# The scan step ahead of the inverse step in each slot of a chunked DeltaNet recurrence

## The chip, the cores and the metric

The kernel runs on one core of a Trainium2 chip. The metric is the time of one execution on the device, in microseconds (us). Three executions of the kernel before took 1556.57, 1556.83 and 1557.63 us; their median, 1556.83 us, is the time to be compared with.

## What is computed

One layer of a hybrid trunk over 1024 tokens of width 1024: RMSNorm, one input projection, a gated DeltaNet mixer with 8 heads beside 4 heads of cross-attention to 256 memory tokens, an output projection, and a SwiGLU feed-forward block of width 2816. The change touches the DeltaNet mixer, whose core in the reference is (cut):

```python
sol = triangular_solve(lower + eye, rhs, lower=True, unit_diagonal=True)   # per chunk
u, w = sol[..., :DV], sol[..., DV:]
def step(state, xs):                       # over the chunks, in order
    v_new = u_n - w_n @ state
    o_n = qg_n @ state + p_n @ v_new
    state = state * gl_n + kg_n.T @ v_new
    return state, o_n
```

The kernel works with chunks of 128 tokens, so that a head has 8 of them. A triangular matrix of each chunk is inverted first (this needs no state); then the chunks of a head are gone through one after the other.

## The kernel before

**Units and iterations.** A unit is one head and one half of the sequence, four chunks; there are 16 units. The loop over `i` runs 20 iterations. In iteration `i` three things stand side by side: the dense input projection for unit `i` (products of 128x128 weights with 128x512 inputs, each done three times with split operands; accumulator `pj`), the inverse of unit `i - 1` (the generator `inverse`), and the recurrence of unit `i - 2` (the generator `scan`). Iterations 2 to 15 have all three; 16 and 17 have no projection of the mixer left.

**Slots.** An iteration is cut into 16 slots. A slot takes one step of `inverse`, one step of `scan`, the small helpers that the table `STEPS` puts there (transposes of keys, values and queries, the chunk systems), one `tap` (a conv multiply-add on VectorE, tile `cv`, L295), and two steps of the projection, which are six 128x512 products on TensorE (one step in iteration 15).

**Steps of `inverse`** (fp16, four chunks at once). Even slots 0 to 10: a product `pz` of 64 columns per chunk, then VectorE masks it into a tile `zlev` (L517). Odd slots 1 to 11: products `pT` (from `zlev`) and `pU`, then VectorE adds them into `T` (L530) and `U` (L532). Slots 12 to 14: products `pe`, `pv`, `pv2` of 128 columns that correct the result to `uf`. Slot 15 has none.

**Steps of `scan`** (fp32, one chunk per four slots). First slot: product `pc` of state and keys, then VectorE makes `r` (L592). Second: product `pc<-r,uf`, then `vn` (L597). Third: product `pc<-vn,kg`, then the new state `st` (L606). Fourth: the output `po`. An fp32 product of 128x128 is two passes on TensorE; the profile shows it as x2. A unit that begins a head has no product in slot 0, one that ends a head none in slot 14.

**What sets the order.** In iterations 2 to 15 the small products are kept on TensorE in the order in which the program issues them (`pinned`), with the projection between them. On VectorE a scheduler places the instructions, but a `tap` goes behind `crit[0]`, the VectorE instruction that `inverse` or `scan` issued last. In iterations 16 and later the scheduler orders TensorE too.

The loop of the slots (L718 to L731, cut):

```python
for s in range(SLOTS):
    if s == SLOTS - 1:
        stage(k_first, i)
    next(inv, None)
    next(scn, None)
    for fn, lag in STEPS.get(s, ()):
        ...
        stage(fn, i + lag)
    if s in TAPS:
        tap()
    for _ in range(per):
        next(work, None)
```

Of the kernel before, what the change touches and what calls it, by code (L numbers as in the profile page):

```python
# [54 lines left out]
def trunk_kernel(ctx: ExitStack, tc: tile.TileContext, a: dict, out: bass.AP):  # L55
# [224 lines left out]
    def conv_silu(ct_i):  # L280

        cb = pp.tile([P, S + 4], F32, tag="cb", name="cb")
        nc.gpsimd.memset(cb[:, 0:4], 0.0)
        cv = pp.tile([P, NT, P], F32, tag="cv", name="cv", bufs=4)
        w = convw[:, ct_i, :]

        def half(hf, pj):
            cf = flat(cv)[:, hf * HF:(hf + 1) * HF]
            nc.scalar.copy(cb[:, 4 + hf * HF:4 + (hf + 1) * HF], pj)
            nc.scalar.activation(cf, pj, AF.Copy, scale=w[:, 3:4])  # L290

            def taps():
                for j in (2, 1, 0):
                    c0 = 1 + j + hf * HF
                    nc.vector.scalar_tensor_tensor(out=cf, in0=cb[:, c0:c0 + HF], scalar=w[:, j:j + 1],  # L295
                                                   in1=cf, op0=ALU.mult, op1=ALU.add)
                    if j == 0:
                        nc.scalar.activation(cf, cf, AF.Silu)
                    yield
            pending.append(taps())  # L300
        return cv, half
# [3 lines left out]
    def tap():  # L305

        while pending:
            with behind():
                if next(pending[0], 0) is None:
                    return  # L310
            pending.pop(0)
# [31 lines left out]
    def dense(jobs):  # L343

        for dst, key, make in jobs:
            whi, wlo = next_w()
            dst[key], half = make()
            for hf in range(2):
                pj = bank("pj", "pj")
                for dt in range(ND):  # L350
                    w, v = whi[:, dt, :], wlo[:, dt, :]
                    x, y = uhi[hf][:, dt, :], ulo[hf][:, dt, :]
                    mm(pj, w, x, start=dt == 0, stop=False)
                    mm(pj, w, y, start=False, stop=False)
                    mm(pj, v, x, start=False, stop=dt == ND - 1)
                    if dt == ND - 1:
                        half(hf, pj)
                    yield
# [287 lines left out]
    def weight_sums(k):  # L646

        def load(i, j):
            t = pp.tile([P, HF], F32, tag="kvo", name="wsum", bufs=3)
            nc.sync.dma_start(t, wo_block(i, j, k))  # L650
            return t

        def put(name, dst, x, y):
            nc.gpsimd.tensor_tensor(out=dst, in0=x, in1=y, op=ALU.subtract)
            nc.sync.dma_start(t_d[name][k], dst)

        b12, b11 = load(1, 2), load(1, 1)
        put("T1", b11, b12, b11)
        b22 = load(2, 2)
        put("T3", b12, b22, b12)  # L660
        put("T2", b22, b22, b11)
        b21 = load(2, 1)
        put("T4", b21, b21, b22)

    def stage(fn, u):
        if 0 <= u < 2 * H:
            return fn(u // 2, u % 2, hd[u // 2], st[u])
# [36 lines left out]
    for i in range(2 * H + 4):  # L704
        h = i // 2
        jobs = []
        if h < H:
            if i % 2 == 0:
                jobs = [(hd[h], "vT", lambda h=h: conv_silu(16 + h)), (hd[h], "qT", lambda h=h: conv_silu(h))]
            else:  # L710
                if h + 1 < H:
                    jobs = [(hd[h + 1], "kT", lambda h=h: conv_silu(9 + h))]
                jobs += [(hd[h], "zs", silu_z)]
        pinned[0] = 2 <= i < 2 * H
        work = dense(jobs)
        per = len(jobs) * 2 * ND // SLOTS
        inv, scn = stage(inverse, i - 1) or iter(()), stage(scan, i - 2) or iter(())
        for s in range(SLOTS):  # L718
            if s == SLOTS - 1:
                stage(k_first, i)  # L720
            next(inv, None)
            next(scn, None)
            for fn, lag in STEPS.get(s, ()):
                if fn is post and i == 2 * H - 1:
                    continue
                if fn is post_y and i >= 2 * H - 1:
                    continue
                stage(fn, i + lag)
                if fn is q_scores and i == 2 * H:
                    with tc.issue_after(st[i - 1]["qk_ins"]):  # L730
                        stage(post_y, i - 4)  # L731
                        stage(post_y, i - 3)
                if fn is k_system and i == 2 * H - 1:
                    with tc.issue_after(st[i]["al_ins"]):
                        stage(post, i - 3)
# [4 lines that stand above are left out]
        for _ in work:  # L740
            pass
        if i % 2 == 1 and 1 <= h <= KH:
            with tc.issue_after(st[i]["al_ins"]), tc.issue_after(st[i]["gr_ins"]):
                weight_sums(h - 1)
# [703 lines left out]
def build(arrays):  # L1448
    import concourse.bacc as bacc

    nc = bacc.Bacc("TRN2", target_bir_lowering=False, num_devices=1)
    aps = {}
    for name, v in arrays.items():
        aps[name] = nc.dram_tensor(f"in_{name}", v.shape, mybir.dt.from_np(v.dtype), kind="ExternalInput").ap()
    out = nc.dram_tensor("out_h", (S, D), F32, kind="ExternalOutput").ap()
    with tile.TileContext(nc) as tc:  # L1456
        trunk_kernel(tc, aps, out)
    return nc
# [9 lines left out]
```

## Time and profile before

| | |
|---|---|
| median of three executions | 1556.83 us |
| the profiled execution, its own time | 1557.43 us |
| its span, first to last instruction | 1555.3 us |
| TensorE (PE) busy over the span | 1477.7 us, 95% |
| VectorE (DVE), ScalarE (ACT), GpSimd (POOL) busy | 69%, 44%, 53% |
| mean granted TensorE clock | 0.986 of full speed |
| iterations 2 to 15 | 130.5 to 614.5 us of the span |

The profiled execution's time is its span and 2.1 us around it. PE counts products, PEld the loading of their stationary operand, which runs beside PE. In a timeline a row is an instruction, or several equal ones (xN), with its start and its length; the starts of pipelined products tell more than their lengths, which overlap. A bracket at a row's end is idle time of the engine just before, and what ended it.

### The profile page before, as it was taken

Reading aid. Unit: us, or ns where it says so; the run is one execution under the profiler, and the core shown is the slowest. Engines: PE = TensorE matmul, PEld = TensorE weight load, DVE = VectorE, ACT = ScalarE, POOL = GpSimd, SP = SyncE. Lnnn points to the kernel's source line nnn. Section 1 sums busy time; section 2 is a strip of 40 time slices with the busy share of each in tenths; the row PEclk is TensorE's granted clock in tenths of the full one; section 3 lists DMA queues with packets and bytes.
Section 4 is the critical chain, followed back from the end, with each engine's and each line's share of the span. In section 5 each row is a group of like instructions: output and inputs, shape, how many; then the busy total and the mean of one; then the engine's idle time right before and its main releaser. Section 6 shows DMA issues by size and latency. Waiting matters only on the chain. (4 is left out here: it accounts for less than half of the span.)

```text
span 1555.3 us, 22654 instructions
## 1 busy us (share of the span) xinstructions
PE 1477.7 (95%) x8237; PEld 1180.3 (76%) x8237; DVE 1067.9 (69%) x1651; ACT 680.4 (44%) x1481; POOL 822.4 (53%) x705
## 2 busy tenths in 40 slices
PE   7999999999999999999898889999999999999996
PEld 5777777777777777887676668877887887778784
DVE  7565766656666757667977886666766766585967
ACT  7464445455454554345346532222222222544352
POOL 3543636464546544204755556666656565544455
PEclk9999999999999999999899899999999999999998
DMA  6411213122212220219334222222222324973334
GB/s 201 156 55 42 77 53 104 68 76 64 85 62 76 76 74 29 82 62 306 108 109 148 81 94 97 102 102 100 103 86 93 112 81 144 317 251 98 93 97 161
DMA packets 77554, 168.13 MB, mean 108 GB/s; under 512 B 10434, under 2 KB 12930, under 8 KB 77443
## 3 DMA queue, kind: packets, MB, share of 16 engines
q1 hardware_dynamic: 76720, 165.58, 31.9%
q8 instruction: 64, 1.05, 0.3%
q10 hardware_dynamic: 722, 1.12, 0.2%
q14 instruction: 48, 0.39, 0.1%
HBM read 124.42 MB, written 42.24 MB: 107 GB/s over the span
## 5 line engine op out<-in xcount | busy, mean ns | idle before, releaser
L246 PE MATMUL pj<-uhi,whi 128*128 128x512 f32 x496 | 215.7, 435 | 0.0
L93 POOL TENSOR_TENSOR wlo<-raw,whi 128x1024 fp32r<-128x1024 f32 x61 | 158.2, 2594 | 74.9 <-ACT whi L92 74.6
L246 PE MATMUL pj<-uhi,wlo 128*128 128x512 f32 x496 | 195.8, 395 | 0.0
L246 PE MATMUL pj<-ulo,whi 128*128 128x512 f32 x496 | 193.7, 391 | 0.0
L1292 POOL TENSOR_TENSOR wlo<-ar,whi 128x512 fp32r<-128x512 f32 x75 | 105.4, 1407 | 99.8 <-ACT whi L1291 99.8
L295 DVE SCALAR_TENSOR_TENSOR cv<-cb,convw_sb,cv 128x512 f32<-128x512 f32 x144 | 132.6, 921 | 24.0 <-ACT cv L290 23.3
L907 PE MATMUL fo<-wlo,whi 128*128 128x512 f32 x308 | 123.0, 399 | 9.4 <-DVE wlo L1292 9.2
L92 ACT CAST whi<-raw 128x1024 fp32r<-128x1024 f32 x66 | 69.6, 1055 | 119.2 <-DVE raw L1057 56.7
L908 PE MATMUL fo<-whi,wlo 128*128 128x512 f32 x308 | 120.6, 392 | 0.0
L906 PE MATMUL fo<-whi 128*128 128x512 f32 x308 | 118.4, 391 | 0.6 <-DVE c L854 0.6
L1095 DVE TENSOR_TENSOR raw<-raw 128x512 f32<-128x512 f32 x86 | 100.3, 1167 | 23.7 <-POOL wlo L93 13.7
L1292 DVE TENSOR_TENSOR wlo<-B,whi 128x512 fp32r<-128x512 f32 x75 | 80.9, 1081 | 45.9 <-ACT whi L1291 45.3
L246 PEld LDWEIGHTS pj<-uhi,wlo 128*128 128x128 f32 x496 | 93.1, 188 | 21.5 <-POOL wlo L93 0.2
L1057 DVE TENSOR_TENSOR raw<-raw,gcols_sb 128x1024 f32<-128x1024 f32 x44 | 64.1, 1457 | 57.9 <-DMA raw<-in_w_ffn_in 57.5
L246 PEld LDWEIGHTS pj<-ulo,whi 128*128 128x128 f32 x496 | 94.2, 190 | 10.8
L246 PEld LDWEIGHTS pj<-uhi,whi 128*128 128x128 f32 x496 | 94.0, 189 | 10.7 <-issue 0.2
L1291 ACT CAST whi<-ar 128x512 fp32r<-128x512 f32 x75 | 46.6, 621 | 113.1 <-POOL wlo L1292 75.4
L530 DVE TENSOR_TENSOR T<-pT,T 128x256 f16<-128x256 f32 x96 | 40.6, 423 | 59.5 <-PE pT L246 58.8
L907 PE MATMUL acc<-wlo,whi 128*128 128x512 f32 x168 | 68.7, 409 | 12.6 <-DVE wlo L891 12.6
L907 PEld LDWEIGHTS fo<-wlo,whi 128*128 128x128 f32 x308 | 58.2, 189 | 29.3 <-DVE wlo L1292 17.7
L1078 POOL TENSOR_TENSOR qlo<-raw,qhi 128x1024 fp32r<-128x1024 f32 x21 | 54.8, 2611 | 42.9 <-ACT qhi L1077 38.5
L517 DVE TENSOR_TENSOR zlev<-pz,lvmask_sb 128x256 f16<-128x256 f32 x96 | 40.4, 421 | 47.1 <-PE pz L246 47.0
(408 smaller groups left out, 4250.9 us busy)
## 6 DMA issues: line engine op xcount, KB each, us to landing
raw<-in_w_ffn_in SPq DMA_DIRECT2D x44, 512.0 KB, 3.3
raw<-in_w_in SPq DMA_DIRECT2D x36, 512.0 KB, 3.2
ar<-g_S SPq DMA_DIRECT2D x44, 256.0 KB, 2.6
B<-in_w_ffn_out SPq DMA_DIRECT2D x42, 256.0 KB, 4.6
g_A<-g SPq DMA_DIRECT2D x33, 256.0 KB, 2.0
ar<-g_A SPq DMA_DIRECT2D x29, 256.0 KB, 3.8
wsum<-in_w_out SPq DMA_DIRECT2D x24, 256.0 KB, 4.3
T_d<-wsum SPq DMA_DIRECT2D x24, 256.0 KB, 2.0
```

Of the source, the lines that this page charges most:

```text
L92: nc.scalar.copy(hi, raw)
L93: (lo_eng or nc.gpsimd).tensor_tensor(out=lo, in0=raw, in1=hi.bitcast(F32), op=ALU.subtract)
L246: ins = nc.tensor.matmul(*args, **kw)
L295: nc.vector.scalar_tensor_tensor(out=cf, in0=cb[:, c0:c0 + HF], scalar=w[:, j:j + 1], in1=cf, op0=ALU.mult, op1=ALU.add)
L906: nc.tensor.matmul(acc[n], hi[:, 0, ts_], hi[:, 1], start=first, stop=False)
L907: nc.tensor.matmul(acc[n], hi[:, 0, ts_], lo[:, 1], start=False, stop=False)
L908: return nc.tensor.matmul(acc[n], lo[:, 0, ts_], hi[:, 1], start=False, stop=last)
L1057: nc.vector.tensor_tensor(out=raw, in0=raw, in1=gcol[:, 1, :].unsqueeze(2).broadcast_to([P, ND, P]), op=ALU.mult)
L1078: nc.gpsimd.tensor_tensor(out=lo, in0=src, in1=hi.bitcast(F32), op=ALU.subtract)
L1095: nc.vector.tensor_tensor(out=o, in0=x, in1=y, op=op)
L1291: nc.scalar.copy(hi[:, i], src)
L1292: last_lo[i] = eng.tensor_tensor(out=lo[:, i], in0=src, in1=hi[:, i].bitcast(F32), op=ALU.subtract).ins
```

## The change

Two lines change places, so that in every slot of every iteration the step of `scan` is issued ahead of the step of `inverse`.

```diff
@@ -718,8 +718,8 @@
         for s in range(SLOTS):
             if s == SLOTS - 1:
                 stage(k_first, i)
+            next(scn, None)
             next(inv, None)
-            next(scn, None)
             for fn, lag in STEPS.get(s, ()):
                 if fn is post and i == 2 * H - 1:
                     continue
```

No instruction is added or taken away. On GpSimd and on the DMA queue of SyncE the order of instructions stays the same. On TensorE, in slot 10 of one iteration, before (`pj` is the projection, `pk` a transpose that a helper issues; the three further pairs of `ah` and `pz` are left out):

```order
L246 MATMUL pj<-uhi_127,wlo 128x512
L246 LDWEIGHTS ah
L246 MATMUL pz<-T,ah 128x64
...
L246 MATMUL pc<-vn,kg 128x128
L250 MATMUL pk<-ident_sb,cv 128x128 x4
L246 MATMUL pj<-uhi_127,whi 128x512
```

On TensorE, the same slot now:

```order
L246 MATMUL pj<-uhi_127,wlo 128x512
L246 MATMUL pc<-vn,kg 128x128
L246 LDWEIGHTS ah
L246 MATMUL pz<-T,ah 128x64
...
L250 MATMUL pk<-ident_sb,cv 128x128 x4
L246 MATMUL pj<-uhi_127,whi 128x512
```

The fp32 product of the scan stood between the fp16 products and the transpose; now it stands between the projection and the fp16 products.

On VectorE, from slot 9 to the start of slot 11 of an iteration, before (`cv` is a tap, `zlev_433` the mask tile of the last level):

```order
L530 TENSOR_TENSOR T<-pT,T 128x8x32
L532 TENSOR_TENSOR U<-pU,U 128x8x32
L295 SCALAR_TENSOR_TENSOR cv<-cb,convw_sb,cv 128x512
L597 TENSOR_SCALAR vn<-pc,beta 128x128
L295 SCALAR_TENSOR_TENSOR cv<-cb,convw_sb,cv 128x512
L517 TENSOR_TENSOR zlev_433<-pz,lvmask_sb 128x4x64
L606 SCALAR_TENSOR_TENSOR st<-st,eg_tot,pc 128x128
```

On VectorE, the same place now:

```order
L597 TENSOR_SCALAR vn<-pc,beta 128x128
L530 TENSOR_TENSOR T<-pT,T 128x8x32
L295 SCALAR_TENSOR_TENSOR cv<-cb,convw_sb,cv 128x512
L532 TENSOR_TENSOR U<-pU,U 128x8x32
L295 SCALAR_TENSOR_TENSOR cv<-cb,convw_sb,cv 128x512
L606 SCALAR_TENSOR_TENSOR st<-st,eg_tot,pc 128x128
L517 TENSOR_TENSOR zlev_433<-pz,lvmask_sb 128x4x64
```

`vn` came behind `T`, `U` and a tap and now leads; `zlev_433` came behind three instructions of the slot before and now has `st` ahead of it too.

## Rows read from the trace of the kernel before

**Rows 1.** Busy time by stage: iterations 2 to 15, then the two after.

```profile
core 0: us, PE busy (x) PEld busy (x) DVE busy (x) ACT busy (x) POOL busy (x), PEclk, DMA share, GB/s
130.50:614.50 484.00, 477.25 (x3580) 379.26 (x3580) 316.44 (x676) 247.04 (x655) 254.65 (x283) 1.00 0.21 70
614.50:645.00 30.50, 30.50 (x258) 25.45 (x255) 19.70 (x50) 10.75 (x43) 11.57 (x17) 1.00 0.22 69
```

**Rows 2.** Waits of PE in 130.5:614.5: us in total, times, longest.

```profile
PE pc L246 <- DVE vn L597: 5.2, 15, 1.0
```

**Rows 3.** Timeline of PE, slots 8 to 11 of one iteration.

```profile
217.45 0.40 PE L246 MATMUL pj<-uhi,wlo 128*128 128x512 f32 x1
...
218.35 0.39 PE L246 MATMUL pj<-ulo,whi 128*128 128x512 f32 x1
...
219.26 0.40 PE L246 MATMUL pj<-uhi,wlo 128*128 128x512 f32 x1
219.50 0.29 PE L246 MATMUL pT<-zlev,U 128*128 128x64 f16 x4
...
221.45 0.29 PE L246 MATMUL pz<-T,ah 128*128 128x64 f16 x4
222.04 0.49 PE L246 MATMUL pc<-vn,kg 128*128 128x128 f32 x2 [0.30 <-DVE vn L597]
...
224.20 0.29 PE L246 MATMUL pT<-zlev,U 128*128 128x64 f16 x4
```

**Rows 4.** Timeline of PE, a slot with transposes (slot 4).

```profile
207.95 0.40 PE L246 MATMUL pj<-uhi,wlo 128*128 128x512 f32 x1
208.19 0.29 PE L246 MATMUL pz<-T,ah 128*128 128x64 f16 x4
208.32 0.47 PE L246 MATMUL pc<-st,khT 128*128 128x128 f32 x2
208.62 0.60 PE L250 MATMUL pvt<-ident_sb,cv 128*128 128x128 f32 x4
...
209.29 0.40 PE L246 MATMUL pj<-ulo,whi 128*128 128x512 f32 x1
```

**Rows 5.** Timeline of PE in iteration 16, where scan precedes inverse.

```profile
623.27 0.39 PE L135 MATMUL pj<-uhi,whi 128*128 128x512 f32 x1
623.50 0.38 PE L246 MATMUL pc<-st,khT 128*128 128x128 f32 x2
623.72 0.39 PE L246 MATMUL po<-st,gr 128*128 128x128 f32 x2
623.94 0.28 PE L246 MATMUL pz<-T,ah 128*128 128x64 f16 x4
...
624.38 0.39 PE L137 MATMUL pj<-uhi,wlo 128*128 128x512 f32 x1
```

**Rows 6.** Timeline of PE in iteration 1: transposes right behind inverse, no scan.

```profile
104.83 0.29 PE L246 MATMUL pz<-T,ah 128*128 128x64 f16 x4
...
105.65 0.39 PE L246 MATMUL pj<-ulo,whi 128*128 128x512 f32 x1
```

**Rows 7.** Timeline of DVE, the stretch of rows 3.

```profile
219.83 0.42 DVE L530 TENSOR_TENSOR T<-pT,T 128x256 f16<-128x256 f32 x1 [1.13 <-PE pT L246]
220.17 0.41 DVE L532 TENSOR_TENSOR U<-pU,U 128x256 f16<-128x256 f32 x1
220.50 1.22 DVE L295 SCALAR_TENSOR_TENSOR cv<-cb,convw_sb,cv 128x512 f32<-128x512 f32 x1
221.64 0.34 DVE L597 TENSOR_SCALAR vn<-pc,beta 128x128 f32<-128x128 f32 x1
221.90 1.38 DVE L295 SCALAR_TENSOR_TENSOR cv<-cb,convw_sb,cv 128x512 f32<-128x512 f32 x1
223.21 0.41 DVE L517 TENSOR_TENSOR zlev<-pz,lvmask_sb 128x256 f16<-128x256 f32 x1
```

**Rows 8.** Timeline of POOL, the stretch of rows 3.

```profile
221.13 1.61 POOL L489 TENSOR_TENSOR al<-at,ah 128x512 f16<-128x512 f32 x1
```

**Rows 9.** All taps (L295): ns min/median/max, first and last start in us.

```profile
L295 DVE SCALAR_TENSOR_TENSOR cv<-cb,convw_sb,cv x144: 735/750/2890, 36.8 to 597.7; 128x512 f32<-128x512 f32 x144
```

## The prediction

> **What bounds the kernel now.** I read the busy times by stage first. In iterations 2 to 15, the only stretch where the two generators run beside the projection on a fixed order, PE is busy for 477.25 of 484.00 us; VectorE is busy for 316.44 us, ScalarE and GpSimd for about half, and the granted clock is 1.00, the 2.4 GHz level [rows 1]. PE is the bound, and time can be won in two ways only: by the 6.75 us in which PE sits idle, and by how closely its products follow each other, which busy time hides, since pipelined products overlap. So the second view is who PE waited for: most of it is one wait, the scan's product `pc<-vn,kg` for the VectorE result `vn`, 15 times, 5.2 us [rows 2]. The third is the timeline of one such wait, with PE and VectorE beside each other [rows 3, 7]. The fourth is the distance from the start of the last dense product of a slot to the second one of the next: I call it the bridge, and it is what the small products cost PE [rows 3 to 6].
>
> **The wait in slot 10.** In slot 9 VectorE does `T`, `U`, a tap and only then `vn`. The tap took 1.22 us where the median tap takes 0.75 [rows 7, 9], so `vn` ended at 221.98 (221.64 + 0.34). In slot 10 PE was at `pz` at 221.45; the scan's product follows a `pz` by 0.13 (208.19 to 208.32 [rows 4]), so it could have started at 221.58 and started at 222.04 [rows 3]. That is 0.46 lost, of which the bracket shows 0.30; the other 0.16 is the modelled tail of `pz`. For 15 waits: 5.2 + 15 x 0.16 = 7.6 us. After the change `vn` stands ahead of `T`. Its product starts 0.23 behind the last dense one (623.27 to 623.50 [rows 5]), at 219.49, and is 0.38 long, so `vn` runs from about 219.91 to 220.25, where PE wants it at 221.43. The margin is over a microsecond. **Term 1: 7.6 us less.**
>
> **The bridges.** Each slot now goes dense, scan, inverse, helpers, dense; it went dense, inverse, scan, helpers, dense. No trace of before shows the new bridge whole in iterations 2 to 15, but its pieces stand in iterations 16 and 1. Dense to scan 0.23; a two-pass fp32 product to the next fp32 product 0.22 (623.50 to 623.72), and from fp32 to `pz` the same 0.22 (623.72 to 623.94); `pz` to the second dense product 0.44 (623.94 to 624.38) [rows 5]; `pz` through four transposes to the second dense product 0.82 (104.83 to 105.65) [rows 6].
> A slot without helpers: before 217.45 to 218.35, 0.90 [rows 3]; after 0.23 + 0.22 + 0.44 = 0.89. A slot with four transposes: before 207.95 to 209.29, 1.34 [rows 4]; after 0.23 + 0.22 + 0.82 = 1.27. The reason shows in one distance: a scan product behind fp16 products takes 0.30 to its successor (208.32 to 208.62 [rows 4]), behind a dense one 0.22 [rows 5]. The loading of its stationary operand is covered by a dense product and not by the short fp16 ones. Afterwards an uncovered load remains, but where transposes follow it is a cheaper one.
> Transposes follow in slots 2, 4, 5 and 10, in 14 iterations less one without a next key: 55 slots x 0.07 = 3.9 us. Of the other eleven slots with an inverse step, slot 0 of seven units and slot 14 of seven have no scan product: 154 - 14 = 140 slots x 0.01 = 1.4 us. The starts are rounded to 0.01, so a slot may be off by 0.02: 0.05 to 0.09 and 0 to 0.03, together 2.8 to 9.2 us. I take the differences as they stand. **Term 2: 5.3 us less.**
>
> The Trainium skill speaks against term 2: "TensorE: Matmul & The Clock Gate", section "Step-by-step: what each phase is for", says that PE pulls the load of a stationary operand ahead of the running matmul, so that the next weights load while this one computes. By that rule alone the order inside a slot would cost nothing and term 2 would be zero. The distances agree with it beside dense products and not beside the fp16 ones of 64 columns.
>
> **A new wait, slot 11.** What was early becomes late: `T` and the mask `zlev` now stand behind the scan's VectorE step. The tightest place is `zlev_433`, which `pT` of slot 11 needs. By rows 7: `vn` holds VectorE for 0.26 (221.64 to 221.90), so `T` starts at 220.17 instead of 219.83; `T` 0.34, tap 1.14 (220.50 to 221.64), `U` 0.33, tap 1.31 (221.90 to 223.21), `st` 0.26 like `vn`, `zlev` 0.41: it ends at 223.96, and PE sees it some 0.06 later (221.98 to 222.04), at 224.02. PE: slot 10 starts at 221.43, lasts 2.75 - 0.46 - 0.07 = 2.22 (221.45 to 224.20 [rows 3], less the wait and the shorter bridge), so slot 11 starts at 223.65; its output product is four passes, 0.44 (623.50 to 623.94 [rows 5]), and `pT` comes at 224.09. The slack is 0.07 us, a knife edge, once in each of 14 iterations. I take 0.5 us in all (some units late by less than 0.1); the ends are 0 and the price in the first rival. **Term 3: 0.5 us more.** Elsewhere the scan's VectorE step delays `T` or `zlev` by no more than 0.34, and `pz` or `pT` needs them most of a slot (219.50 to 221.45 [rows 3]) later.
>
> **What costs nothing.** The tap stays behind the last step of the slot, whichever generator issued it. GpSimd and the DMA queue keep their order, and PE waits for neither of them here; GpSimd's 254.65 us fit into a stage of 471 as well. In iterations 16 and 17 the scheduler orders anew, but PE was busy for all of 30.50 us [rows 1], with projection products of the memory heads as filler; I allow 1 us either way. Behind them PE's program is as before and the whole is 95% PE, so what is won arrives at the end.
>
> **The sum.** -7.6 - 5.3 + 0.5 = -12.4 us. The profiled execution took 1557.43 us, which gives 1545.0; it is 0.6 above the median, so against that I predict **1544.4 us**, 0.8% less.
>
> **The rivals.**
> *Late mask.* The two taps run beside GpSimd's `al` (221.13 to 222.74 [rows 8]) and were 0.47 and 0.63 longer than the median. If their new place costs another 0.47 (what the first one lost), `zlev_433` is 0.40 late: 14 x 0.40 = 5.6 in place of 0.5, so 1549.5. For it: the margin of 0.07. Against: the second tap starts only 0.08 later, and `al` ends while it runs. The Trainium skill, "SBUF — State Buffer", section "SBUF: two separate sides", says that the port pair shared by VectorE and GpSimd is an exclusive lock and the loser blocks for the whole instruction. By it the second tap would start when `al` ends, at 222.74, and end 0.2 later than I have it: 14 x 0.13 = 1.8 us for term 3, 1545.7. The first tap, 0.75 of work done in 1.22 while GpSimd was busy throughout, speaks against a full block. Chance 0.18, with all between.
> *The loads are covered anyway.* Term 2 is zero, because scan products behind dense ones wait for something that iteration 16 doesn't show: 1556.83 - 7.6 + 0.5 = 1549.7. The distances of [rows 5, 6] speak against it. Chance 0.09. The rule of the Trainium skill named under term 2 ends at the same time.
> *The change doesn't do what it says.* The order of PE shows that it does; but if both the wait merely moves (from `vn` to `zlev_433`, 0.46 each) and the bridges stay, nothing is left: 1556.8. Chance 0.04.
> *VectorE becomes the bound: slower.* Place: the two taps between slots 9 and 11. Taps of up to 2.89 us occur [rows 9]. If the second took that long instead of 1.38, `zlev_433` would be 1.51 - 0.07 = 1.44 late in each unit: +20.2 - 12.9 = +7.3, 1564.1. It turns from a gain to a loss at (7.6 + 5.3) / 14 + 0.07 = 1.0 us of lateness. Against: VectorE has 167 us free in the stage, and nothing on GpSimd grows. Chance 0.04.
>
> **How the numbers follow.** The forecast, with its rounding (2.8 to 9.2 in term 2), has 0.65. The range goes from 1541.5 (term 2 at 8) to 1550.5, which takes in the late mask and the covered loads; it leaves out the last two rivals and the far ends. A difference under 0.2% (3.1 us) can't be told from none. Faster by more than that: 0.65 + 0.18 + 0.09 - 0.01 for a double mishap = 0.91; within: 0.05; slower: 0.04.
>
> **What would show it.** Right: the wait for `vn` gone from PE's list; bridges of 1.27 in slots 2, 4, 5 and 10; the stage 130.5 to 614.5 shorter by some 12 us and what follows as long as before. Term 1 is wrong if another wait of about 0.4 stands in slot 10 or 11; term 2 if the bridges with transposes are still 1.34; term 3 shows as PE waiting for `zlev` L517 fourteen times. If the stage wins 12 us and the end doesn't, the gain was given back behind 645.

## The result, and the profile after

| | before | after |
|---|---|---|
| median of four executions each | 1557.07 us | 1535.97 us |
| lowest and highest | 1556.57, 1557.63 | 1533.81, 1536.47 |
| the profiled execution's span | 1555.3 us | 1533.7 us |

The ratio is 0.9866, with an interval of 0.9837 to 0.9896: 21.1 us less, 1.3%. The forecast was 12.4 less, and the time lies below its range. To see where the other 9 us come from, I cut both spans at the starts of the same products:

| stretch of the span, us | before | after | difference |
|---|---|---|---|
| up to iteration 2 | 127.4 | 129.1 | +1.7 |
| iterations 2 to 15 | 487.1 | 476.2 | -10.9 |
| iterations 16 and 17, memory attention | 84.5 | 83.6 | -0.9 |
| output projection (`acc`) | 155.0 | 153.6 | -1.4 |
| from there to the FFN loop | 42.8 | 41.9 | -0.9 |
| FFN loop, first product of `T3` to first `fo` | 420.5 | 412.4 | -8.1 |
| output of the FFN | 238.0 | 237.0 | -1.0 |

(The cut of iterations 2 to 15 begins 3 us ahead of that in the table of before, so it is 487 and not 484.) The stage of the forecast gave 10.9 us and the two iterations behind it 0.9, near the 12.4 of the forecast. The surprise lies 300 us behind them, in a loop that the change doesn't touch.

**The stage of the slots, after.** Busy time by stage (us; each engine's busy time and instructions, granted clock, DMA share, GB/s), to be laid beside [rows 1]:

```profile
core 0: us, PE busy (x) PEld busy (x) DVE busy (x) ACT busy (x) POOL busy (x), PEclk, DMA share, GB/s
132.20:605.20 473.00, 470.42 (x3583) 405.95 (x3582) 331.70 (x676) 246.05 (x655) 256.05 (x283) 1.00 0.22 72
605.20:634.80 29.60, 29.60 (x256) 24.87 (x254) 20.17 (x50) 10.50 (x42) 11.59 (x17) 1.00 0.21 67
```

Here 11.0 us are gone, 4.2 of them idle time of PE, the rest in the distances that busy time hides. All waits of PE in that stretch (us in total, times, longest), beside [rows 2]:

```profile
PE pz L246 <- DVE T L530: 1.6, 1, 1.6
PE pT L246 <- DVE zlev L517: 0.7, 1, 0.7
PE pc L246 <- DVE vn L597: 0.2, 1, 0.2
```

The fifteen waits for `vn` are one, and `zlev` is waited for once and not fourteen times. The timeline of PE, slots 8 to 11 of the same iteration as in [rows 3] (start, length):

```profile
216.90 0.40 PE L246 MATMUL pj<-uhi,wlo 128*128 128x512 f32 x1
217.13 0.39 PE L246 MATMUL pc<-st,khT 128*128 128x128 f32 x2
217.35 0.28 PE L246 MATMUL pz<-T,ah 128*128 128x64 f16 x4
...
217.78 0.40 PE L246 MATMUL pj<-ulo,whi 128*128 128x512 f32 x1
...
220.65 0.39 PE L246 MATMUL pj<-uhi,wlo 128*128 128x512 f32 x1
220.87 0.38 PE L246 MATMUL pc<-vn,kg 128*128 128x128 f32 x2
221.09 0.28 PE L246 MATMUL pz<-T,ah 128*128 128x64 f16 x4
221.21 0.63 PE L250 MATMUL pk<-ident_sb,cv 128*128 128x128 f32 x4
...
221.91 0.39 PE L246 MATMUL pj<-ulo,whi 128*128 128x512 f32 x1
...
223.05 0.38 PE L246 MATMUL po<-st,gr 128*128 128x128 f32 x2
...
223.50 0.28 PE L246 MATMUL pT<-zlev,U 128*128 128x64 f16 x4
```

The bridge of slot 8 is 216.90 to 217.78, 0.88; that of slot 10, with its transposes, 220.65 to 221.91, 1.26. VectorE beside it:

```profile
219.37 0.35 DVE L597 TENSOR_SCALAR vn<-pc,beta 128x128 f32<-128x128 f32 x1 [1.13 <-PE pc L246]
219.64 0.41 DVE L530 TENSOR_TENSOR T<-pT,T 128x256 f16<-128x256 f32 x1
219.97 1.20 DVE L295 SCALAR_TENSOR_TENSOR cv<-cb,convw_sb,cv 128x512 f32<-128x512 f32 x1
...
222.92 0.41 DVE L517 TENSOR_TENSOR zlev<-pz,lvmask_sb 128x256 f16<-128x256 f32 x1
```

`vn` is done at 219.72, 1.1 us before PE wants it (220.87). The mask ends at 223.33 and `pT` starts at 223.50; the knife edge of the forecast held.

**The FFN loop, before and after.** The waits of PE for the low half `qlo` of the next weights, 900 to 1330 us, first in before, then in after:

```profile
PE sc L137 <- POOL qlo L1078: 10.8, 7, 3.5
```

```profile
PE sc L137 <- POOL qlo L1078: 3.5, 1, 3.5
```

Of the 8.1 us of the loop 7.3 are in this one wait. The groups of line L1095, four VectorE steps per block that combine the weights, same stretch (count | busy us, mean ns | idle time ahead and what ended it), before and then after:

```profile
L1095 DVE TENSOR_TENSOR raw<-raw 128x512 f32<-128x512 f32 x80 | 94.9, 1186 | 23.4 <-POOL wlo L93 13.7 <-POOL wlo L1078 8.6
```

```profile
L1095 DVE TENSOR_TENSOR raw<-raw 128x512 f32<-128x512 f32 x80 | 79.4, 992 | 25.4 <-POOL wlo L93 17.1 <-POOL wlo L1078 7.1
```

The same 80 instructions, on the same data, in a loop whose order is the same on every engine in both traces, take 15.5 us more in before. One block of each shows why. Before, VectorE and GpSimd:

```profile
976.55 0.69 DVE L854 TENSOR_TENSOR c<-g,v 128x512 f32<-128x512 f32 x1 [1.19 <-POOL g L854]
977.16 2.90 DVE L1095 TENSOR_TENSOR raw<-raw 128x512 f32<-128x512 f32 x1
979.99 0.68 DVE L854 TENSOR_TENSOR u<-iv,m 128x512 f32<-128x512 f32 x1
...
976.58 2.93 POOL L1078 TENSOR_TENSOR plo<-raw,phi 128x1024 fp32r<-128x1024 f32 x1
983.87 3.07 POOL L1078 TENSOR_TENSOR qlo<-raw,qhi 128x1024 fp32r<-128x1024 f32 x1 [4.36 <-PE pj L137]
```

After:

```profile
965.07 0.68 DVE L1095 TENSOR_TENSOR raw<-raw 128x512 f32<-128x512 f32 x1
965.67 0.68 DVE L854 TENSOR_TENSOR u<-iv,m 128x512 f32<-128x512 f32 x1
...
965.73 2.42 POOL L1078 TENSOR_TENSOR plo<-raw,phi 128x1024 fp32r<-128x1024 f32 x1 [1.30 <-ACT phi L1077]
969.56 2.40 POOL L1078 TENSOR_TENSOR qlo<-raw,qhi 128x1024 fp32r<-128x1024 f32 x1 [1.41 <-ACT qhi L1077]
```

In before the fourth step of L1095 starts 0.58 us behind GpSimd's `plo`, takes 2.90 us instead of 0.68 and ends 0.55 behind it; `u<-iv,m`, which PE's next products need, comes 2.2 us later. In after the fourth step has just ended when `plo` starts. I call such a meeting a collision. In before 7 of the 18 blocks behind block 3 have one of over 2 us, and the starts of `plo` follow each other by anything from 18.2 to 23.0 us, mostly 18.4 and 21.3 in turn; in after there is none, and they follow each other by 19.2 us, block for block. Seven collisions for 8.1 us of loop are 1.2 us each. So the question for the experiments was: does the slot order cause the collisions, or does it only happen to go with them?

### The profile page after: what moved, and what is told of

Its sections match the earlier page's. It is cut to its first block, busy times and chain, and to the rows that moved or that the text cites. A ratio compares the mean times of both kernels' runs of the same rounds, so it can differ in the third digit from the quotient of the medians.

```text
span 1533.7 us, 22655 instructions
## 1 busy us (share of the span) xinstructions
PE 1468.6 (96%) x8237; PEld 1207.5 (79%) x8237; DVE 1068.4 (70%) x1651; ACT 682.1 (44%) x1481; POOL 825.6 (54%) x705
## 3 DMA queue, kind: packets, MB, share of 16 engines
q8 instruction: 64, 1.05, 0.3%
## 4 chain that ended last, share of the span: by engine, by line
PE 35%; DVE 5%; POOL 4%; issue 3%; DMA 2%; ACT 2%; DVEq 0%; SPq 0%; POOLq 0%; ACTq 0%
PE fo L907 3%; PE fo L908 3%; PE fo L906 3%; PE sc L137 3%; PE sc L135 2%; PE sc L136 2%; PE iv L135 2%; PE iv L137 2%; PE iv L136 2%; PE pj L136 2%; PE pj L137 2%; PE pj L135 2%; POOL wlo L891 2%; DVE B L854 1%; PE ms L136 1%
## 5 line engine op out<-in xcount | busy, mean ns | idle before, releaser
L295 DVE SCALAR_TENSOR_TENSOR cv<-cb,convw_sb,cv 128x512 f32<-128x512 f32 x144 | 148.3, 1030 | 23.1 <-ACT cv L290 22.4
L1095 DVE TENSOR_TENSOR raw<-raw 128x512 f32<-128x512 f32 x86 | 84.8, 986 | 25.6 <-POOL wlo L93 17.1
L1057 DVE TENSOR_TENSOR raw<-raw,gcols_sb 128x1024 f32<-128x1024 f32 x44 | 67.2, 1527 | 50.0 <-DMA raw<-in_w_ffn_in 50.0
L1078 POOL TENSOR_TENSOR plo<-raw,phi 128x1024 fp32r<-128x1024 f32 (+1 forms) x22 | 52.7, 2397 | 46.2 <-ACT phi L1077 44.8
L908 PE MATMUL acc<-whi,wlo 128*128 128x512 f32 x168 | 68.7, 409 | 2.4 <-POOL wlo L891 2.4
L906 PEld LDWEIGHTS fo<-whi 128*128 128x128 f32 x308 | 58.2, 189 | 13.5 <-DVE c L854 1.0
```

Source lines behind the costliest of these rows:

```text
L906: nc.tensor.matmul(acc[n], hi[:, 0, ts_], hi[:, 1], start=first, stop=False)
L908: return nc.tensor.matmul(acc[n], lo[:, 0, ts_], hi[:, 1], start=False, stop=last)
L1095: nc.vector.tensor_tensor(out=o, in0=x, in1=y, op=op)
```

## The parts of the slot order

Iterations 2 to 15 took 487.0 to 487.1 us in all seven traces with the old order, and 476.1 to 476.3 in all six with the new one, whatever else differed. So a single trace resolves some two tenths of a us here.

**Slots 9 and 10 only, and all but these.** The edits of the loop:

```diff
-            next(inv, None)
-            next(scn, None)
+            for step in (scn, inv) if s in (9, 10) else (inv, scn):
+                next(step, None)
```

and the same with `s not in (9, 10)`.

> Scan ahead of inverse in slots 9 and 10 alone. My terms: the wait for vn goes (7.6 us) and 13 or 14 slots 10 have the shorter bridge (0.07 each, 0.9) and 14 slots 9 (0.01): iterations 2 to 15 are 8.6 us shorter. Rival (the wait only moves, to zlev_433, and the gain of iterations 2 to 15 is all from the bridges): 1 us shorter. Behind them, by theory A, either nothing or another 10 us, by how TensorE enters the feed-forward loop; by theory B a part of 9.5 us.

> Scan ahead of inverse in all slots but 9 and 10. My terms: the wait for vn in slot 10 stays; 42 slots with transposes x 0.07 = 2.9 and some 126 others x 0.01 = 1.3: iterations 2 to 15 are 4.2 us shorter. If the bridges are worth nothing (loads covered anyway): 0. Behind them as in the run with slots 9 and 10: by theory A nothing or 10 us, by theory B a part.

Measured: 483.9 and 484.4 us for the stage, 3.2 and 2.7 less than before; together 5.9, while all slots at once give 10.9. The expectations, 8.6 and 4.2 less, were both missed. In the second run the bridges of iterations 2 to 14 are 4.3 us shorter by their starts, but the dense products between them take 1.3 us more than in before. Waits of PE in the stage, slots 9 and 10 only:

```profile
PE pT L246 <- DVE zlev L517: 2.3, 13, 0.2
```

and all but 9 and 10:

```profile
PE pc L246 <- DVE vn L597: 4.4, 14, 0.3
```

The second is the old wait, as it should be. The first is new: with slot 11 in its old order, PE comes to `pT` without the output product ahead of it, 0.44 us sooner, and `zlev_433` isn't ready. From the prediction's own numbers (slack 0.07) PE is then kept for 0.37, in 14 iterations 5.2 us: just the missing 5.0. If that is so, slot 11 alone must bring it back:

```diff
+            for step in (scn, inv) if s in (9, 10, 11) else (inv, scn):
```

> The scan step first in slots 9, 10 and 11 only. Slots 9 and 10 alone took 3.2 us off iterations 2 to 15, all others alone 2.7, together 10.95. Theory D: in slots 9 and 10 alone PE reaches pT in slot 11 without the output product ahead of it, 0.44 us sooner, and waits there for zlev_433 (0.37 by the prediction's numbers, 14 times, 5.2 us). With slot 11 changed as well this wait goes: iterations 2 to 15 take 8.0 to 9.0 us less than before, no wait of PE for zlev. Rival E (the wait goes by what the other slots bring): 3 to 4 us less, and the waits for zlev and st stay. With an FFN loop as before the time is 1548 to 1550 by D and 1553 to 1555 by E; the loop may differ by 8 us for itself.

Measured: 479.4 us, 7.75 less than before, 0.25 short of the range of theory D; no wait for `zlev` is left, and slot 11 is worth 4.5 us. Its whole time, 1540.58, was 8 us under the expectation, because its FFN loop was a short one (412.5). So the change in slots 9 and 10 pays only with slot 11, and the wait that "merely moves" of the prediction's rivals is real where slot 11 is left out.

## The FFN loop

**PE shifted at the loop's entry.** In the first two blocks PE did three products more, in the old order, or three less, in the new one (the output then lacks a part of the FFN):

```diff
-        m7 = prod("iv" if k else "pj", w["S3"], T3)
+        m7 = prod("iv" if k else "pj", w["S3"], T3, again=3 * (k < 2))
```

`again` starts the first product of `m7` anew so many times, without changing the result.

> Old slot order. In the feed-forward loop, blocks 0 and 1, the first product of the group for m7 is issued three times more (its sum is started anew, the result is the same): TensorE comes 3 x 0.23 = 0.7 us later in each, 1.4 us in all; every other engine keeps its instructions and order. Theory A (the feed-forward loop has two rhythms, and how far TensorE lags the element-wise chain when it enters the loop chooses between them): the loop falls into the rhythm that the new kernel has, GpSimd's wait-for-lo of TensorE (qlo, seven waits in the old kernel) goes to about one, and the time is 1557 + 1.4 - 9 to 11 = 1547 to 1550. Theory B (the gain behind the recurrence comes from the slot order in some other way): 1557 + 1.4 = 1558.4, the qlo waits stay.

> New slot order. In the feed-forward loop, blocks 0 and 1, the last three products of the group for m7 are left out (that part of the sum is missing): TensorE comes 0.7 us earlier in each, 1.4 us in all. Theory A: the loop falls into the rhythm of the old kernel, the qlo waits come back, and the time rises by some 10 us in spite of the missing work: 1536 - 1.4 + 9 to 11 = 1543 to 1546. Theory B: 1534.6, one qlo wait.

Measured: 1551.79 us with a loop of 412.3 in the old order, and 1537.15 with 411.0 in the new one. The first shows that the old order can have the short loop, but not that the three products brought it: its stretch at the low clock at the loop's entry was 6.8 us, and with such a one unedited loops are short too (the table further down). The second missed its expectation, the long loop didn't come back. There `plo` of block 4 started 0.01 us behind the end of the fourth step, just not in collision.

**One disturbance.** Three kernels shifted one engine once, in one block: ScalarE casts `phi` twice in block 4 (old order), PE repeats a product five times in block 2 (old order), VectorE does two idle steps in block 4 (new order):

```diff
+            for _ in range(times):      # times = 2 for phi, k == 4
+                nc.scalar.copy(hi, src)
```

```diff
+        m7 = prod("iv" if k else "pj", w["S3"], T3, 5 * (k == 2))
```

```diff
+        for _ in range(2 * (k == 4)):
+            nc.vector.tensor_tensor(out=g[:, 4:], in0=g[:, 4:], in1=g[:, 4:], op=ALU.max)
```

> Slot order as before. In one block of the FFN loop (k = 4) ScalarE casts phi twice, so GpSimd's plo starts 1.05 us later, behind the end of the VectorE step L1095 (956.1 to 957.7 in the trace of before, where plo started at 957.3). Everything else is as before, but for one L1057 one place later on VectorE. Theory A (the FFN loop has a rhythm in which plo and qlo run beside two-input VectorE steps, and one in which they don't; whichever is entered keeps itself up): the FFN loop takes 412 to 414 us instead of 420.55, the waits of PE for qlo fall from 7 to at most 2, the time is 1549 to 1551. Theory B (the loop's length follows from what PE does in each block, or from the granted clock at its entry): 420 us, 1558.

> Slot order as before. In block 2 of the FFN loop PE starts the products of m7 with the first one done five times more (1.07 us of PE work, the result unchanged), so PE frees phi 1.07 us later for block 4, behind the half-clock stretch at the loop's entry. Theory A (the rhythm of plo and VectorE's L1095): the loop takes 412 to 415 us with the extra 1.07 included, 1549.5 to 1552. Theory B (the clock at the entry, or PE's own work, sets it): 421.6 us, 1559.

> Slot order as after. In one block of the FFN loop (k = 4) VectorE does two more two-input steps on 128x512 (the maximum of a tile with itself, which changes nothing) behind the last L1095, 945.6 on, so VectorE is some 1.4 us later and plo, at 946.5, runs beside them. Theory A: the loop falls into the other rhythm and stays in it: 418 to 422 us instead of 412.4, PE waits for qlo 5 to 7 times, 1542 to 1545. Theory B (a single disturbance is made up for within a block or two): 412 to 414 us, 1536 to 1538.

Measured: 1560.36, 1549.49 and 1541.10 us; loops of 423.1, 413.5 and 416.7. And the kernel before, run beside them, took 1551.02, 5.5 us under its lowest until then. The first went the wrong way by theory A: with `phi` 1.05 later block 4 had no collision (`plo` 1.6 us behind the fourth step), but block 5 had, and seven more followed. So 1 us on one engine in one block can turn a loop of 412 into one of 423. The second came out as theory A had it, but `plo` of block 4 stood there at the same 1.6 us behind the fourth step as in the first: where `plo` stands in one block doesn't settle the loop by itself. The third shows that the long form need not keep itself up: it had collisions in blocks 4 and 5, and from block 7 on went at 19.2 like the undisturbed one. All three had 6.8 us at the low clock at the entry, so the first and the third disturbed a loop that would have been short, and the second is no test of PE's shift. Theory A was thus right on what the loop is sensitive to, and wrong on how firmly either form holds.

**Both kernels again, several executions.** The run of 1551 said that my four executions of before were too alike to tell its spread. On one chip:

> The kernel before once more, unchanged. In its first trace the FFN loop took 420.55 us, with plo (GpSimd) running beside the fourth step of L1095 (VectorE) in every other block; one execution of it beside the last experiments took 1551.02 us where five others took 1556.57 to 1559.69. Theory A (the FFN loop has two rhythms; which one a run enters is decided by some tenths of a us at its entry, and the half-clock stretch there, 3.4 us long where the loop was slow and 6.8 where it was fast, is part of that): the times fall into two groups, 1549 to 1552 and 1556 to 1560, and the trace shows the loop at 411 to 414 or 419 to 423 to match, iterations 2 to 15 at 487.0 in either. Rival B (the slot order alone puts the loop into its slow rhythm): all at 1556 to 1560, the loop at 420.

> The kernel after once more, unchanged. Theory A (two rhythms, chance at the entry): most at 1534 to 1537 with a loop of 411 to 414, and where a run falls into the slow rhythm 1541 to 1545. Rival B (the slot order sets the rhythm): all at 1533 to 1537. Both: iterations 2 to 15 at 476.1.

Measured: before 1546.0 to 1563.3 us, median 1556.9 of 35, with 18 above 1556 (the two sets of it, of ten and of 25, have medians of 1550.9 and 1557.3, so a median of ten isn't firm either); after 1535.8 to 1552.3, median 1542.9 of 10. Ten against the 25 that stood beside them give a ratio of 0.9925, interval 0.9891 to 0.9960. Rival B falls: the new order too has its long loop, 419.7 us in the profiled execution of this set (424.2 in the one of before), with the stage at 476.1 as ever. The times don't fall into two clean groups as theory A had it. The long loops differ in their number of collisions (five in this trace of after, nine in this one of before), but not in that alone: the three traces with seven took 418.8, 420.5 and 422.2.

**The collision taken away.** From block 2 on the fourth step goes to GpSimd, which does it ahead of `plo`, so the two can't meet. PE keeps its order:

```diff
-            nc.vector.tensor_tensor(out=o, in0=x, in1=y, op=op)
+            (nc.gpsimd if n == 3 and k > 1 else nc.vector).tensor_tensor(out=o, in0=x, in1=y, op=op)
```

(`n` counts the four steps.)

> Slot order as before. In the FFN loop from k = 2 on the fourth step of L1095 goes to GpSimd, ahead of plo, so the two can't run beside each other any more; PE's order is unchanged. Theory A: the slow rhythm has lost its cause: the loop takes 411 to 415 us, PE waits for qlo at most twice, 1548 to 1552 whatever the kernel before does on this chip. Rival B (the overlap of plo and L1095 is a sign and not the cause): the loop stays at 419 to 423, 1556 to 1560. Rival C (GpSimd gets too long, 1.3 to 1.7 us a block more): PE waits for qlo in every block, 425 us or more.

> Slot order as after, and the fourth step of L1095 on GpSimd from k = 2 on. Theory A: the FFN loop is 411 to 415 us in this one and in the same edit on the old order, so the difference of the two is the slot order alone: 11 us in iterations 2 to 15 and 1 to 3 behind them, 12 to 14 us together; 1535 to 1538. Rival B: the difference stays 21 us, since the slot order itself changes the loop.

Measured: 1548.86 us in the old order (1546.0 to 1553.2, ten executions), 1535.86 in the new one (1535.5 to 1538.5, four); loops of 412.6 and 412.4 us, one wait for `qlo`. Both traces had 6.8 us at the low clock at the entry, with which the loop is short without the edit as well, so these two loops are no test. The times are: none of the ten executions in the old order took more than 1553.2, where 18 of the 35 of before on the same chip took more than 1556. So with the collision the long loop goes. The traces agree: in all sixteen, a loop with a collision of over 2 us took 416.7 us or more, one without 413.5 or less. What is left between the two medians, of ten and of four, is put down to the slot order: 13.0 us. The new order with this edit also has the lowest median of the kernels that were run several times on this chip; that the spread of after, 16 us, is gone can't be told from four executions, since the first four of after lay as close.

**What decides which loop comes.** Two traces of the old order, one of the kernel as it is and one in which PE does six products more (1.28 us) in block 2:

```diff
+        m7 = prod("iv" if k else "pj", w["S3"], T3, 6 * (k == 2))
```

> Slot order as before; in block 2 of the FFN loop the first product of m7 is done six times more (1.28 us of PE work, result unchanged, order of all engines unchanged). Theory A (an execution enters the slow rhythm if PE is early against VectorE at block 3, and the short half-clock stretch makes it early): no slow executions are left, all at 1547 to 1554, where the kernel before spreads from 1546 to 1563 with some half of its executions above 1556. Rival B (PE's lateness doesn't decide, something else that goes with the clock does): the same two groups as before, shifted by the 1.28, some half of the executions above 1557.

> Slot order as after, and the same six products more. Theory A: no slow executions are left, all at 1534 to 1541, where the kernel after spread from 1535.8 to 1552.3 over ten; the median is 12 to 14 us under that of the same edit on the old order. Rival B: the spread stays, half of the executions above 1542.

Timeline at block 4, the kernel before as it is:

```profile
955.78 2.40 DVE L1095 TENSOR_TENSOR raw<-raw 128x512 f32<-128x512 f32 x2
...
956.55 1.06 ACT L1077 CAST phi<-raw 128x1024 fp32r<-128x1024 f32 x1 [4.31 <-DVE raw L1095]
957.68 2.76 POOL L1078 TENSOR_TENSOR plo<-raw,phi 128x1024 fp32r<-128x1024 f32 x1
```

and with the six products:

```profile
955.78 2.38 DVE L1097 TENSOR_TENSOR raw<-raw 128x512 f32<-128x512 f32 x2
...
957.65 1.06 ACT L1079 CAST phi<-raw 128x1024 fp32r<-128x1024 f32 x1 [5.41 <-PE sc L136]
958.78 2.42 POOL L1080 TENSOR_TENSOR plo<-raw,phi 128x1024 fp32r<-128x1024 f32 x1 [1.17 <-DVE u L854]
```

VectorE is at the same place to 0.01 us. In the first the cast of `phi` waits for VectorE, PE had freed its buffer 0.3 us before, and `plo` starts 0.5 us ahead of the end of the fourth step (957.68 against 955.78 + 2.40), which here costs `plo` 0.3 us (2.76 against 2.42); the first fourth step of 2.9 us comes in block 5. In the second PE is later, the cast waits for it, and `plo` starts 0.6 behind. The loops: 424.2 and 411.9 us. Over ten executions this kernel took 1543.9 to 1555.2, median 1549.0, where before took 1547.7 to 1564.3, median 1556.8 of 14 beside it; the top went 1 us over theory A's bound. The new order with the same edit: 1537.7 to 1540.2, median 1539.9 of five, loop 412.3; the two medians differ by 9.1, where 12 to 14 were expected. These two are the only edited loops with the 3.4 us of the long ones at the low clock, and both are short. So PE being *later* at the entry makes the loop shorter, by 7 to 12 us against the long loops of the same order.

Without an edit, whether PE is late goes with the clock. Granted clock (the figure ahead of the last two) at the entry of the loop, in this trace of before:

```profile
927.30:930.70 3.40, 2.89 (x7) 2.31 (x8) 1.76 (x2) 0.42 (x1) 0.45 (x1) 0.50 0.91 301
930.70:934.10 3.40, 3.40 (x17) 2.77 (x16) 2.86 (x3) 1.25 (x2) 3.25 (x2) 0.99 0.21 80
```

and in the first trace of after:

```profile
914.80:918.20 3.40, 2.77 (x7) 2.21 (x8) 1.63 (x2) 0.29 (x1) 0.58 (x1) 0.50 0.90 312
918.20:921.60 3.40, 3.40 (x10) 2.66 (x9) 2.83 (x3) 1.38 (x2) 3.12 (x2) 0.50 0.22 82
921.60:925.00 3.40, 3.40 (x16) 2.81 (x15) 3.40 (x2) 0.00 (x0) 3.20 (x2) 0.99 0.17 60
```

Ahead of these stretches PE had been idle for most of the time (busy for 0.79 of 4.30 us, and for 1.07 of 4.80). It then runs at the 1.2 GHz level for 3.4 us in the one and 6.8 in the other, where the second stretch has 10 products instead of 17, some 1.6 us of work less. All traces of unedited loops, and the two with the six products:

| slot order | at 1.2 GHz at the entry, us | `plo` of block 4 behind the fourth step, us | loop, us |
|---|---|---|---|
| old, first trace | 3.4 | -0.43 | 420.5 |
| old, second trace | 3.4 | -0.49 | 424.2 |
| 9 and 10 only | 3.4 | -0.48 | 422.2 |
| all but 9 and 10 | 3.4 | -0.49 | 418.8 |
| new, second trace | 3.4 | -0.49 | 419.7 |
| new, first trace | 6.8 | +0.88 | 412.4 |
| slots 9 to 11 | 6.8 | +0.47 | 412.5 |
| old, six products more | 3.4 | +0.62 | 411.9 |
| new, six products more | 3.4 | +0.78 | 412.3 |

The column of `plo` goes with the loop in all nine, the slot order doesn't. That the length of the clock stretch sets PE's place is read from seven traces without an exception, and not shown by an edit; the last two rows show that PE's place is enough. The seven traces that are not in the table, all with an edit in the loop, had 6.8 us, and their loops were short but for the two in which ScalarE or VectorE was delayed in block 4. What sets the length was not tried.

## Why the prediction was right in its stage and wrong on the whole

**Term 1, the wait for `vn` (7.6 less): right.** In the 13 slots 10 read in both traces the bridge went from 1.83 (median) to 1.27, 0.56 less; 0.07 of that is term 2, which leaves 0.49 a slot, 6.4 in all, where the prediction had 0.46. Two of the fifteen waits lay elsewhere: one in a slot 6, where the bridge was 1.15 over its median, of which nothing is left, and one in a slot 2, 0.94 over it, where 0.51 is left. Together 8.0.

**Term 2, the bridges (5.3 less): right in its mechanism, 5.7 in size.** Start to start, the median bridge with four transposes went from 1.34 to 1.28 in slot 2, from 1.34 to 1.27 in slot 4, from 1.45 to 1.39 in slot 5: with slot 10 some 3.8, as forecast. In slot 5, however, six of fourteen took 1.48 to 1.55: there the load of the scan's product waits for `r`, which VectorE now delivers just too late (waits of PEld, iterations 2 to 15),

```profile
PEld pc L246 <- DVE r L592: 1.8, 6, 0.3
```

and PE loses some 0.14 each time, 0.8 us. The prediction spoke of `T` and `zlev` as what becomes late, and not of the scan's own operands being wanted earlier. The plain slots gained 0.02 and not 0.01 (0.90 to 0.88, 1.02 to 1.00, 1.24 to 1.22), 2.8 us and not 1.4: starts of two digits were too coarse a ruler. The rule of the Trainium skill that stood against this term ("TensorE: Matmul & The Clock Gate", section "Step-by-step: what each phase is for": the next weights load while this product runs) holds here beside the dense products, and not behind the 64-column fp16 ones: had it held for all, these bridges would not have moved.

**Term 3, `zlev_433` (0.5 more): nothing, which is one end of its bounds.** No slot 11 of after has a wait for it; in the shown iteration the slack was 0.17 (223.33 to 223.50, where the prediction had 0.07 + 0.06). So the late mask and the VectorE-bound rival are out. The runs of slots 9 and 10 with and without 11 show that the edge is real: 4.5 us hang on that output product. The one wait for a `zlev` in the list of after lies elsewhere, in slot 7 of iteration 3,

```profile
180.35 0.28 PE L246 MATMUL pT<-zlev,U 128*128 128x64 f16 x4 [0.74 <-DVE zlev L517]
```

and makes that bridge 0.9 longer than the others of slot 7. In before the same iteration had its wait one slot earlier, the 1.15 of term 1: most of it was only moved. A tap that waits for ScalarE holds up VectorE there in both kernels. The prediction had "Elsewhere the scan's VectorE step delays `T` or `zlev` by no more than 0.34", and so no cost.

**The late mask, misread.** The prediction took the first tap, "0.75 of work done in 1.22 while GpSimd was busy throughout", as a sign against a full block. [rows 8] show `al` alone, but GpSimd's work before it ended during this tap:

```profile
218.78 2.40 POOL L93 TENSOR_TENSOR wlo<-raw,whi 128x1024 fp32r<-128x1024 f32 x1 [0.36 <-ACT whi L92]
```

The tap ended at 221.72, 0.55 behind the end of `wlo` (221.17), and the second tap at 223.28, 0.54 behind the end of `al` (222.74). Both waited until GpSimd was done, so a full block is what the rows show. The 0.2 that this would cost by the prediction is too much because it puts all 0.75 of a tap behind the release, where 0.55 was measured.

**The sum.** -10.9 in the stage, in every trace, and -0.9 in iterations 16 and 17 (84.5 in the seven traces of the old order, 83.6 in the six of the new), for which the prediction allowed 1 us either way: -11.8 against -12.4. In the stage the terms give -8.0 - 5.7 + 0.9 (the bridge in slot 7), some 2 us more than was won, so that the sum came out so near is in part luck; 1.1 of that are dense products, which follow each other by 0.2309 us on average in after and by 0.2296 in before, over 850 of them, and most of the rest lies in iteration 15, which as a whole won 0.07. Why is open. With the collision taken away from both, the two orders differ by 13.0 us; with PE made later in both, by 9.1. Why this last one is smaller isn't settled: in its two traces the output projection, where the granted clock falls at varying places, differed by 1.4 us, and 2.8 in the output of the FFN, both against the new order, while the stage differed by the usual 10.9.

**The step that failed** is "Behind them PE's program is as before and the whole is 95% PE, so what is won arrives at the end", and with it "what follows as long as before". PE's program is as before, but the same program behind it takes 411 to 424 us in the FFN loop, in either order. In the first comparison the profiled execution of before had a long loop and that of after a short one, and the times of each lay within 3 us, so the loop added some 8.1 us to the gain; over more executions of both the medians differ by 13.9 (and by the ratio above, 0.9925, by 11.7), near the forecast. The trace of before did hold the warning: PE's waits for `qlo`, 10.8 us in seven, and a fourth step of L1095 at 0.68 in one block and 2.90 in the next, in a loop whose blocks are all alike. I read neither, since the change doesn't reach there. And I took 1 us of repeat spread for the precision of the whole, where three executions had all landed in the same form of the loop.

## What to carry to other kernels

Where a loop of equal blocks shows unequal blocks in the profile (18.4 and 21.3 us in turn here), it is in a rhythm that a microsecond at its entry can change, and any edit ahead of it is then timed together with that: look for such a loop first, and give the range its two lengths. To time an edit, compare the stretch that it touches between the same two products in both traces (here 487.1 against 476.2, to 0.2), or take the rhythm away in both, and only then the ends. When two interleaved chains are swapped, swap through to the place where the later one is next wanted: slots 9 and 10 gave 3.2 us alone and 7.75 with slot 11.

## What was not expected of the hardware

- A two-input VectorE step on 128x512 fp32 took 0.68 us by itself and 2.90 beside a GpSimd subtraction of 128x1024, longer than the 2.42 which that subtraction takes alone. Of "SBUF — State Buffer", section "SBUF: two separate sides", in the Trainium skill (an exclusive lock; the loser blocks for the whole instruction) the traces here agree for VectorE steps with both inputs in SBUF. In all seven collisions of before the fourth step ends 0.55 us behind the end of `plo` (980.06 against 979.51), as do the taps that start while a `wlo` or an `al` of GpSimd runs. GpSimd is held in the same way: `plo` took 2.93 because VectorE's `c<-g,v` had started 0.03 us ahead of it and kept its 0.69.
- A longer stretch at the low clock went with a faster kernel: 3.4 us more at 1.2 GHz cost PE some 1.6 us, and the loops with it were 6 to 12 us shorter (412.4 and 412.5 against 418.8 to 424.2). Six needless products (1.28 us) brought the short loop too.
- With the fourth step on GpSimd, 1.30 us a block more there, GpSimd's sum grew and the loop still took 412 us: what mattered was when it was busy, not how long.
